# A decoder trunk on one core: another bank for the last half-columns, roots on ScalarE, residual sums as accumulating transfers, stores per row tile

## The chip, the core and the metric

The kernel runs on one core of one Trainium2 chip. The metric is the device time of one execution in microseconds; the median of several runs counts. TensorE (PE) multiplies, VectorE (DVE), ScalarE (ACT) and GpSimd (POOL) work on elements, and transfers are issued from the queues of SyncE (SP), ScalarE and GpSimd.

## The reference, cut to what matters

One layer, 512 tokens, 1024 channels, all in fp32. The parts that the change touches are the second norm, the down-projection with its residual sum, and the final norm:

```python
x = x + gate1 * (merged @ w_out[l])
h2 = _rmsnorm(x, norm2_g[l]) * (1.0 + scale2) + shift2
x = x + gate2 * _conv_ffn(h2, w_up[l], conv_w[l], conv_b[l], w_down[l])
...
return _rmsnorm(x, final_g)
```

`_rmsnorm` multiplies by `rsqrt(mean(x*x) + 1e-6)` and by a gain. `_conv_ffn` multiplies by w_up (1024 x 5632), puts a causal convolution of width 3 and a GELU on one half, multiplies by the other half, and multiplies by w_down (2816 x 1024).

## The kernel before

Every fp32 product is made of three: both operands are split into a rounded high part (cast on ScalarE) and the remainder (subtraction on VectorE; both in `split`, L101), and high by high, high by low and low by high are summed in PSUM.

The 512 tokens are four row tiles of 128. `x1` holds their residual stream in SBUF, [128, 4, 1024]. The up-projection and the down-projection are each done as seven block products instead of eight (a Strassen-like scheme), so sums and differences of blocks are needed as operands and of products afterwards. `mul_slot` (L1043) does the up-projection; the last 120 us are the down-projection.

The down-projection runs seven passes (L1473): m1, m5, m6, p2, p3, m7, p4. Each pass goes over the 2816 inner rows in six groups, five of two blocks and one of one (`grp`, L1420; NG = 6). For each group, `prepare` (L1626) splits the pass's operands: `ax` (pool tag gx, 5 buffers) and `wh`, `wl` (tags whi, wlo, WB = 3 buffers each). For some passes it also issues, on GpSimd, a transfer that adds another weight block onto the raw one (`accum_op=ALU.add`), for a later pass. Then `multiply` (L1642) does the products for u = 0 and 1, the two row tiles of one token half, into the pass's pair of PSUM banks: dX, dZ, dY, dW. A bank is 128 x 512.

`after_pass` (L1508) is a generator of small steps that turn finished banks into residual sums: subtract a bank, multiply by the gate, add to `x1`, take the square's row sum on ScalarE (`square`, L1485; its sum goes to `parts`), multiply by the final gain. The table `EACH` (L1658) says how many such steps are traced behind each group's `prepare` in the next pass. So steps from p2 run during p3, those from p3 during m7, those from m7 during p4. `e`, `e2` and `m1` are the buffers of differences.

The order of the instructions on VectorE, ScalarE, GpSimd and, here, TensorE is set by a planner that goes by the order of tracing and its own estimate of durations. Inside a `manual_schedule` block the order is that of the text. Two such blocks matter. The first (L1183 to L1380) holds the end of the output projection, the second norm and the start of the up-projection: `square2` (L1119), `norm_a` (L1125), `norm_b` (L1129). The second is `last_rows` (L1587): the last three groups (HOLD = 3) of the last pass, p4, and everything after them. There, TensorE finishes u = 0, then u = 1 in two column halves `c0` and `c1` of 256, both in bank dW[1]. `last_mul`, `last_add`, `last_gain`, `last_scale` and `last_scale2` (L1562 to L1585) turn the banks into output rows; `last_scale2` scales the second 512 columns on ScalarE and stores them from the queue that it is given.

The inverse root of a mean square is `rstd_start` (L136: the mean on VectorE, power -0.5 on GpSimd) and `rstd_end` (L146: a correction step in two VectorE instructions). The signs are arranged by factors -0.5 in the gains. The only activation tables needed before are those of Exp and Tanh, and from L1066 on that of Gelu.

Every engine, and every queue of transfers, takes its instructions in order: what waits holds up what stands behind it.

Of the kernel before, what the change touches and what calls it, by code (L numbers as in the profile page):

```python
# [8 lines left out]
F32 = mybir.dt.float32  # L9
# [5 lines left out]
P = 128  # L15
D = 1024
S = 512
# [26 lines left out]
def kernel(  # L44
# [101 lines left out]
    def rstd_end(dst, ms, r0, n, wpool):  # L146
        t = wpool.tile([P, n], F32, tag="rs_b", bufs=3, name="rt")
        if n == 1:
            nc.vector.scalar_tensor_tensor(t, r0, r0, ms, ALU.mult, ALU.mult)
        else:  # L150
            nc.vector.tensor_mul(t, r0, r0)
            nc.vector.tensor_mul(t, t, ms)
        nc.vector.scalar_tensor_tensor(dst, t, -3.0, r0, ALU.add, ALU.mult)

# [701 lines left out]
    while units or loaded or current or later:  # L856
        fill(1)
    for _ in ada:
        fill(1)
# [259 lines left out]
    def square2(t, hfs=(0, 1)):  # L1119
        for hf in hfs:  # L1120
            sq = big.tile([P, S], F32, tag="sq2", name=f"sqo{t}{hf}")
            ssq[t, hf] = bp.tile([P, 1], F32, tag="ss2", bufs=8, name=f"sso{t}{hf}")
            nc.scalar.activation(sq, x1[:, t, hf * S : (hf + 1) * S], AF.Square, accum_out=ssq[t, hf])  # L1123

    def norm_a(t):  # L1125
        nc.vector.tensor_scalar(ssq[t, 0], ssq[t, 0], 1.0 / D, EPS, ALU.mult, ALU.add)
        r2[t] = rstd_start(ssq[t, 1], 1, D, bp, plus=ssq[t, 0])

    def norm_b(t):  # L1129
        rs = bp.tile([P, 1], F32, tag="rs2", bufs=4, name=f"rso{t}")  # L1130
        rstd_end(rs, *r2[t], 1, bp)
        xns[t] = xnp[t // 2][:, t % 2]
        return rs
# [285 lines left out]

    grp = [(p, min(p + 2, NPR)) for p in range(0, NPR, 2)]  # L1420
# [70 lines left out]
    def stat_start(t):  # L1491
        a, b = parts[t, 0], parts[t, 1]
        nc.vector.tensor_scalar(a, a, 1.0 / D, EPS, ALU.mult, ALU.add)
        parts[t] = rstd_start(b, 1, D, bp, plus=a)

    def stat_end(t):
        rs = bp.tile([P, 1], F32, tag="rs2", bufs=4, name=f"rsd{t}")
        rstd_end(rs, *parts[t], 1, bp)
        return rs
# [8 lines left out]
    def after_pass(name):  # L1508
# [14 lines left out]
        elif name == "m7":  # L1523
# [4 lines left out]
            for u in two:  # L1528
                def add(u=u):
                    V.tensor_add(res(2 + u, 1), res(2 + u, 1), e2[:, u])  # L1530
                    square(2 + u, 1)
                yield add
            for u in two:
                def gain(u=u):
                    V.tensor_mul(e2[:, u], res(2 + u, 1), fgb[:, S:])
                    stat_start(u)
                yield gain
        elif name == "p3":
# [4 lines left out]
            for u in two:  # L1543
                def add(u=u):
                    V.tensor_add(res(u, 1), res(u, 1), e[:, u])
                    square(u, 1)
                yield add
            for u in two:
                yield lambda u=u: V.tensor_mul(res(u, 1), res(u, 1), fgb[:, S:])
        elif name == "p2":  # L1550
            for u in two:
                yield lambda u=u: V.tensor_mul(m1[:, u], dX[u], gate(0))
            for u in two:
                def add(u=u):
                    V.tensor_add(res(u, 0), res(u, 0), m1[:, u])
                    square(u, 0)
                yield add
# [4 lines left out]
    def last_mul(u, sl=slice(0, S)):  # L1562
        nc.vector.tensor_mul(m1[:, u, sl], dW[u][:, sl], gate(0)[:, sl])

    def last_add(u, sl=slice(0, S)):
        nc.vector.tensor_add(res(2 + u, 0)[:, sl], res(2 + u, 0)[:, sl], m1[:, u, sl])
        sq = big.tile([P, S], F32, tag="sq2", name=f"sqe{u}_{sl.start}")
# [19 lines left out]
    def last_rows(todo):  # L1587
# [8 lines left out]
        for sl in (c0, c1):  # L1596
            for g in todo:
                multiply(len(passes) - 1, g, 1, sl)
        for u in range(2):
            nc.scalar.activation(x1[:, u], x1[:, u], AF.Copy, scale=stat_end(u))  # L1600
# [41 lines left out]
    def multiply(i, g, u, sl=slice(0, S)):  # L1642
# [4 lines left out]
        for q in range(n):  # L1647
            first_mm = name in first and g == 0 and q == 0
            last_mm = g == len(grp) - 1 and q == n - 1
            for x, (a, b) in enumerate(((ah, wh), (ah, wl), (al, wh))):  # L1650
                nc.tensor.matmul(  # L1651
                    bank2[u][:, sl], a[:, q, cu], b[:, q, sl], start=first_mm and x == 0, stop=last_mm and x == 2,
                    skip_group_check=name not in first,
                )
# [65 lines left out]
```

## Time and profile before

| | us |
|---|---|
| runs shown: median (lowest to highest), 3 runs | 695.13 (693.9 to 696.05) |
| the profiled execution's own time | 695.11 |
| its span, first to last instruction | 693.3 |
| mean granted TensorE clock | 0.995 |
| TensorE busy | 676.6 (98%) |
| VectorE busy | 559.9 (81%) |
| ScalarE busy | 376.6 (54%) |
| GpSimd busy | 72.7 (10%) |

A row of the timeline gives the start in us from the span's beginning, the duration, the engine, the line of the program, the operation, output and inputs by name, the shapes, the number of instructions merged in the row, and in brackets the idle time just before with what ended it. A row of the chain gives start, length and whose time it is; "issue" is time in which nothing visible was waited for. A row of transfers gives target and source, the issuing queue, the count, the size of each and the median time from issue to landing. A "q" behind an engine's name is its sequencer.

### The profile page before, as it was taken

The page shows a single profiled execution, that of the slowest core. Times are in us where ns is not written, and L with a number is a line of the kernel's source. Part 1 is how long each engine was busy: PE and PEld are TensorE (multiplying, and loading weights), DVE is VectorE, ACT ScalarE, POOL GpSimd, SP SyncE. Part 2 cuts the span into 40 slices and gives each one's busy share as a digit, 9 for nine tenths or more (in the row PEclk, how much of TensorE's full clock was granted, in tenths as well). Part 3 has the DMA queues.
Part 4 walks back from the last instruction along what each step waited for, and adds up shares of the span by engine and source line. Part 5 has one row for each costly group of instructions (what it writes and reads, how often), then busy time and mean ns, then how long its engine had stood idle before and what let it go on. Part 6 is the DMA issues. An engine that isn't in the chain of part 4 may idle for free. (4 is left out here: it accounts for less than half of the span.)

```text
span 693.3 us, 10915 instructions
## 1 busy us (share of the span) xinstructions
PE 676.6 (98%) x4117; PEld 591.5 (85%) x4117; DVE 559.9 (81%) x1028; ACT 376.6 (54%) x661; POOL 72.7 (10%) x81
## 2 busy tenths in 40 slices
PE   8999999999999999999999999999999999999994
PEld 8787777778787888888799999999999998888873
DVE  4888887879787566663699898888888999979995
ACT  4656765354544333332487655665556565665663
POOL 2000000000100000000030101111111003431200
PEclk9999999999999999999999999999999999999997
DMA  9943544355254464258354988778867558996803
GB/s 351 407 166 108 185 134 151 122 172 158 97 178 156 142 222 152 93 186 245 115 108 133 217 212 197 188 194 185 204 172 185 140 177 204 196 205 182 144 1 122
DMA packets 71077, 119.68 MB, mean 173 GB/s; under 512 B 3952, under 2 KB 47728, under 8 KB 71024
## 3 DMA queue, kind: packets, MB, share of 16 engines
q1 hardware_dynamic: 52960, 95.04, 41.4%
q0 software_dynamic: 17776, 23.60, 20.6%
q8 instruction: 32, 0.52, 0.3%
q10 hardware_dynamic: 288, 0.34, 0.1%
q14 instruction: 21, 0.17, 0.1%
HBM read 116.87 MB, written 2.10 MB: 172 GB/s over the span
## 5 line engine op out<-in xcount | busy, mean ns | idle before, releaser
L1051 PE MATMUL up<-t,m_whi 128*128 128x256 f32 x528 | 96.1, 283 | 0.0
L1051 PEld LDWEIGHTS up<-t,m_whi 128*128 128x128 f32 x528 | 82.3, 192 | 0.0
L1051 PE MATMUL up<-t,m_wlo 128*128 128x256 f32 x264 | 74.6, 283 | 0.1
L1051 PE MATMUL up<-bh,p_wlo 128*128 128x256 f32 x232 | 65.7, 284 | 0.7 <-DVE p_wlo L994 0.7
L1051 PE MATMUL up<-bh,p_whi 128*128 128x256 f32 x232 | 65.6, 283 | 0.0
L1051 PE MATMUL up<-bl,p_whi 128*128 128x256 f32 x232 | 65.6, 283 | 0.0
L673 DVE CUSTOM_DVE_ANT_0 ra<-ra,csb 128x1024 f32<-128x1024 f32 x32 | 39.1, 1223 | 23.5 <-DMA ra<-in_w_ada_t_dram 23.2
L1051 PEld LDWEIGHTS up<-t,m_wlo 128*128 128x128 f32 x264 | 50.6, 192 | 0.3 <-DVE m_wlo L994 0.3
L1051 PEld LDWEIGHTS up<-bh,p_wlo 128*128 128x128 f32 x232 | 44.4, 192 | 1.1 <-DVE p_wlo L994 1.1
L1051 PEld LDWEIGHTS up<-bh,p_whi 128*128 128x128 f32 x232 | 44.5, 192 | 0.0
L1051 PEld LDWEIGHTS up<-bl,p_whi 128*128 128x128 f32 x232 | 44.5, 192 | 0.0
L962 POOL DMA_DIRECT2D s<-in_w_up_dram x21 | 27.1, 1363 | 156.0 <-DMA s<-in_w_up_dram 109.4
L143 POOL TENSOR_TENSOR r<-ms,mhalf 128x1 f32<-128x1 f32 (+1 forms) x13 | 11.8, 910 | 297.9 <-DVE ms L139 220.8
L994 DVE TENSOR_TENSOR m_wlo<-s,m_whi 128x1024 fp32r<-128x1024 f32 x31 | 37.8, 1220 | 2.0 <-ACT m_whi L990 2.0
L990 ACT CAST m_whi<-s 128x1024 fp32r<-128x1024 f32 x31 | 32.4, 1046 | 9.3 <-DVE s L984 6.0
L612 ACT ACTIVATE sd<-sd,dmx 128x128 f32<-128x128 f32 (+3 forms) x32 | 17.8, 556 | 29.8 <-DVE dmx L610 24.0
L1051 PE MATMUL up<-t,p_whi 128*128 128x256 f32 x176 | 32.2, 283 | 0.0
L1051 PEld LDWEIGHTS up<-t,p_whi 128*128 128x128 f32 x176 | 27.4, 192 | 0.2 <-issue 0.2
L1058 ACT ACTIVATE gT<-a,cols 128x512 f32<-128x512 f32 x22 | 17.7, 813 | 17.7 <-DVE a L1093 17.3
L990 ACT CAST p_whi<-wa 128x1024 fp32r<-128x1024 f32 x18 | 18.7, 1041 | 12.0 <-DMA s<-in_w_up_dram 8.9
L1051 PE MATMUL up<-t,p_wlo 128*128 128x256 f32 x88 | 24.9, 283 | 0.0
L994 DVE TENSOR_TENSOR p_wlo<-wa,p_whi 128x1024 fp32r<-128x1024 f32 x18 | 22.0, 1222 | 3.5 <-ACT p_whi L990 3.0
(497 smaller groups left out, 2010.0 us busy)
## 6 DMA issues: line engine op xcount, KB each, us to landing
ra<-in_w_ada_t_dram SPq DMA_DIRECT2D x32, 512.0 KB, 3.3
wa<-in_w_up_dram SPq DMA_DIRECT2D x22, 512.0 KB, 4.4
s<-in_w_up_dram SPq DMA_DIRECT2D x21, 512.0 KB, 4.7
s<-in_w_up_dram POOLq DMA_DIRECT2D x21, 512.0 KB, 6.1
adaw<-in_w_ada_t_dram SPq DMA_DIRECT2D x15, 512.0 KB, 9.8
a<-in_w_up_dram SPq DMA_DIRECT2D x11, 512.0 KB, 4.8
b<-in_w_down_dram SPq DMA_DIRECT2D x10, 512.0 KB, 4.3
w<-in_w_first_dram SPq DMA_DIRECT2D x8, 512.0 KB, 10.1
```

The source lines that it names most:

```text
L143: nc.gpsimd.tensor_tensor(r0, ms, mhalf[:, :n], ALU.pow)
L612: nc.scalar.activation(pm[m], pm[m], AF.Exp, bias=mx[:, m : m + 1], scale=slope, accum_out=lsum[:, m : m + 1])
L673: nc.vector.tensor_tensor_reduce(r, r, csb, 1.0, 0.0, ALU.mult, ALU.add, late_mod[:, idx : idx + 1])
L962: nc.gpsimd.dma_start(dst, upblock(*blk), accum_op=ALU.add)
L990: nc.scalar.copy(W[J, name][0], R[J, SRC[name]])
L994: nc.vector.tensor_sub(lo, R[J, SRC[name]], hi.bitcast(F32))
L1051: nc.tensor.matmul(o[u], w[:, k, cu], b[:, k], start=name in ("p1", "m5", "p2") and k == 0 and x == 0, stop=k == 3 and x == 2, skip_group_ ...
L1058: nc.scalar.activation(grow(j), av[J][:, u], AF.Identity, bias=cv[:, 66 + j : 67 + j], scale=cv[:, 44 + j : 45 + j])
```

## The change

- `root_start` and `root_end` are new: ScalarE's Sqrt of the mean square, then VectorE's reciprocal, then the same correction step. They take the place of GpSimd's power in the second norm (`norm_a`, `norm_b`), in the final norm of row tiles 0 and 1 (`stat_start`, `stat_end`) and in the tail. In the second norm the small `tensor_scalar` on the first half's sum moves from `norm_a` into `square2`, right behind its square.
- `root_table` is new: a Sqrt on one column, once behind the attention's last merge, once behind the last tile of the up-projection, which makes ScalarE load the root's table there.
- Six additions to `x1` on VectorE become transfers on GpSimd's queue that add onto `x1`; the squares follow them.
- In m7, groups 4 and 5 are multiplied first for u = 0 and then for u = 1; in p4 groups 0 and 1 likewise.
- In p4, groups 4 and 5 are followed by three steps instead of two: the two new ones (`row`) scale and store row tiles 0 and 1, which `last_rows` did.
- In `last_rows`, the last three groups of the columns `c1` of u = 1 are summed in bank dY[1]; dW[1] is multiplied and added over its whole width when `c0` is done, and `c1` is added afterwards. Row tile 2 is finished and stored between the two.

```diff
+    def root_start(ssq, d, wpool, plus):
+        r0 = wpool.tile([P, 1], F32, tag="rs_c", bufs=3, name="r0")
+        nc.scalar.activation(r0, ssq, AF.Sqrt, bias=plus, scale=1.0 / d)
+        ms = wpool.tile([P, 1], F32, tag="rs_a", bufs=3, name="ms")
+        nc.vector.scalar_tensor_tensor(ms, ssq, 1.0 / d, plus, ALU.mult, ALU.add)
+        return ms, r0
+
+    def root_end(dst, ms, r0, wpool):
+        nc.vector.reciprocal(r0, r0)
+        rstd_end(dst, ms, r0, 1, wpool)
+
+    def root_table(behind):
+        nc.scalar.activation(warm, behind, AF.Sqrt, scale=0.0)
...
+    root_table(tds[KT - 1][:, 0:1])
...
             nc.scalar.activation(sq, x1[:, t, hf * S : (hf + 1) * S], AF.Square, accum_out=ssq[t, hf])
+            if hf == 0:
+                nc.vector.tensor_scalar(ssq[t, 0], ssq[t, 0], 1.0 / D, EPS, ALU.mult, ALU.add)
 
     def norm_a(t):
-        nc.vector.tensor_scalar(ssq[t, 0], ssq[t, 0], 1.0 / D, EPS, ALU.mult, ALU.add)
-        r2[t] = rstd_start(ssq[t, 1], 1, D, bp, plus=ssq[t, 0])
+        r2[t] = root_start(ssq[t, 1], D, bp, ssq[t, 0])
...
+    root_table(grow(FT - 1)[:, 0:1])
...
                 def add(u=u):
-                    V.tensor_add(res(2 + u, 1), res(2 + u, 1), e2[:, u])
+                    nc.gpsimd.dma_start(res(2 + u, 1), e2[:, u], accum_op=ALU.add)
                     square(2 + u, 1)
                 yield add
             for u in two:
                 def gain(u=u):
+                    stat_start(u)
                     V.tensor_mul(e2[:, u], res(2 + u, 1), fgb[:, S:])
-                    stat_start(u)
                 yield gain
+            for u in two:
+                def row(u=u):
+                    nc.scalar.activation(x1[:, u], x1[:, u], AF.Copy, scale=stat_end(u))
+                    nc.sync.dma_start(od[u * P : (u + 1) * P, :], x1[:, u])
+                yield row
...
-                    V.tensor_add(res(u, 1), res(u, 1), e[:, u])
+                    nc.gpsimd.dma_start(res(u, 1), e[:, u], accum_op=ALU.add)
...
-                    V.tensor_add(res(u, 0), res(u, 0), m1[:, u])
+                    nc.gpsimd.dma_start(res(u, 0), m1[:, u], accum_op=ALU.add)
...
         for g in todo:
             multiply(len(passes) - 1, g, 0)
-        for sl in (c0, c1):
-            for g in todo:
-                multiply(len(passes) - 1, g, 1, sl)
-        for u in range(2):
-            nc.scalar.activation(x1[:, u], x1[:, u], AF.Copy, scale=stat_end(u))
-            nc.sync.dma_start(od[u * P : (u + 1) * P, :], x1[:, u])
-        last_mul(0)
-        s0 = last_add(0)
-        last_gain(0)
-        last_mul(1, c0)
-        r0 = rstd_start(s0, 1, D, bp, plus=part[0])
-        s1 = last_add(1, c0)
-        last_gain(1, c0)
+        for g in todo:
+            multiply(len(passes) - 1, g, 1, c0)
+        for g in todo:
+            multiply(len(passes) - 1, g, 1, c1, dY[1], g == todo[0])
+        last_mul(0, dW[0])
+        last_add(0)
+        s0 = last_square(0)
+        last_mul(1, dW[1])
+        r0 = root_start(s0, D, bp, part[0])
         rs0 = bp.tile([P, 1], F32, tag="rs2", bufs=4, name="rse0")
-        rstd_end(rs0, *r0, 1, bp)
+        root_end(rs0, *r0, bp)
+        last_add(1)
+        last_scale2(0, rs0, nc.sync)
+        s1 = last_square(1, c0)
+        nc.vector.scalar_tensor_tensor(res(2, 0), res(2, 0), rs0, fgb[:, :S], ALU.mult, ALU.mult)
+        nc.sync.dma_start(od[2 * P : 3 * P, :S], res(2, 0))
+        last_mul(1, dY[1], c1)
+        last_add(1, c1)
+        s2 = last_square(1, c1)
         partial(s1, part[1])
-        last_mul(1, c1)
-        s2 = last_add(1, c1)
-        r1 = rstd_start(s2, 1, D, bp, plus=s1)
-        last_gain(1, c1)
-        last_scale(0, rs0)
-        last_scale2(0, rs0, nc.sync)
+        last_gain(1)
+        r1 = root_start(s2, D, bp, s1)
         rs1 = bp.tile([P, 1], F32, tag="rs2", bufs=4, name="rse1")
-        rstd_end(rs1, *r1, 1, bp)
+        root_end(rs1, *r1, bp)
         last_scale(1, rs1)
         last_scale2(1, rs1, nc.scalar)
...
-    EACH = {3: (0, 2, 2, 2, 1, 1), 4: (0, 0, 1, 1, 2, 2), 5: (0, 0, 2, 2, 2, 2), 6: (0, 0, 2, 2, 2, 2)}
+    EACH = {3: (0, 2, 2, 2, 1, 1), 4: (0, 0, 1, 1, 2, 2), 5: (0, 0, 2, 2, 2, 2), 6: (0, 0, 2, 2, 3, 3)}
...
+        together = {"m7": (4, 5), "p4": (0, 1)}.get(passes[i][0], ())
         for g in range(NG - tail):
             for u in range(2):
-                multiply(i, g, u)
+                for gg in together if g in together[:1] else () if g in together else (g,):
+                    multiply(i, gg, u)
```

`last_add` loses its square, which becomes `last_square`; `last_mul` takes the bank, and `multiply` takes an optional bank and a flag that starts it afresh.

More of the change, by code (lines that the diff above doesn't have):

```diff
@@ L1493, in stat_start @@
         nc.vector.tensor_scalar(a, a, 1.0 / D, EPS, ALU.mult, ALU.add)
-        parts[t] = rstd_start(b, 1, D, bp, plus=a)
+        parts[t] = root_start(b, D, bp, a)
     def stat_end(t):
         rs = bp.tile([P, 1], F32, tag="rs2", bufs=4, name=f"rsd{t}")
-        rstd_end(rs, *parts[t], 1, bp)
+        root_end(rs, *parts[t], bp)
         return rs
@@ L1559, in after_pass, with last_mul, last_square @@
                 yield lambda u=u: V.tensor_mul(res(u, 0), res(u, 0), fgb[:, :S])
-    def last_mul(u, sl=slice(0, S)):
-        nc.vector.tensor_mul(m1[:, u, sl], dW[u][:, sl], gate(0)[:, sl])
+    def last_mul(u, src, sl=slice(0, S)):
+        nc.vector.tensor_mul(m1[:, u, sl], src[:, sl], gate(0)[:, sl])
     def last_add(u, sl=slice(0, S)):
         nc.vector.tensor_add(res(2 + u, 0)[:, sl], res(2 + u, 0)[:, sl], m1[:, u, sl])
+    def last_square(u, sl=slice(0, S)):
         sq = big.tile([P, S], F32, tag="sq2", name=f"sqe{u}_{sl.start}")
@@ L1640, in prepare, with multiply @@
         ops[i, g] = ah, al, wh, wl
-    def multiply(i, g, u, sl=slice(0, S)):
+    def multiply(i, g, u, sl=slice(0, S), o=None, fresh=False):
         name, bank2 = passes[i][:2]
@@ L1647, in multiply @@
         for q in range(n):
-            first_mm = name in first and g == 0 and q == 0
+            first_mm = (name in first and g == 0 or fresh) and q == 0
             last_mm = g == len(grp) - 1 and q == n - 1
@@ L1651, in multiply @@
                 nc.tensor.matmul(
-                    bank2[u][:, sl], a[:, q, cu], b[:, q, sl], start=first_mm and x == 0, stop=last_mm and x == 2,
-                    skip_group_check=name not in first,
+                    (bank2[u] if o is None else o)[:, sl], a[:, q, cu], b[:, q, sl], start=first_mm and x == 0, stop=last_mm and x == 2,
+                    skip_group_check=name not in first and o is None,
                 )
```

2 lines of the change are left out of this document (1 added, 1 removed).

## The prediction, made before the changed kernel ran

> **What bounds the kernel now.** I read the chain of waits first, from its end backwards, because it says which engine each stretch is worth anything on.
>
> ```profile
> 393.81 184.34 PE up L1051 x1534
> 578.15 89.12 PE dc L1651 x393
> 667.27 0.02 issue
> 667.29 0.70 DVE chain_outl L1525
> 667.99 0.14 issue
> 668.13 15.45 PE dc L1651 x81
> ...
> 687.16 0.66 POOLq L1716
> ...
> 688.29 0.72 ACT x L1584
> ```
>
> From 393.81 to 667.27 TensorE is the chain without a break. Whatever VectorE, ScalarE or GpSimd save there is worth nothing, and whatever they lose counts only once TensorE stands still. There is one small hole, where pass p4 waits for VectorE's subtraction from its bank (667.29). At 668.13 + 15.45 = 683.58 TensorE is done, and a serial tail of 5.4 us follows to 688.29 + 0.72 = 689.01, then the last store. So the change can gain in the tail, at the hole, and before 393.81, and it can lose anywhere. Next, the tail in the timeline:
>
> ```profile
> 680.01 0.69 DVE L1563 TENSOR_TENSOR pairs<-dc,g2row 128x512 f32<-128x512 f32 x1
> 679.69 2.20 ACT L1600 ACTIVATE x<-x,rsd 128x1024 f32<-128x1024 f32 x2 [1.79 <-DVE rsd L153]
> 681.79 0.62 ACT L1569 ACTIVATE sqe<-x 128x512 f32<-128x512 f32 x1
> 683.60 0.42 DVE L1563 TENSOR_TENSOR pairs<-dc,g2row 128x256 f32<-128x256 f32 x1 [1.44 <-PE dc L1651]
> 685.37 0.41 DVE L1563 TENSOR_TENSOR pairs<-dc,g2row 128x256 f32<-128x256 f32 x1
> 686.34 0.42 ACT L1569 ACTIVATE sqe<-x 128x256 f32<-128x256 f32 x1 [1.25 <-DVE x L1566]
> 686.66 0.19 ACT L1569 ACTIVATION_READ_ACCUMULATOR sqe<-x 128x1 f32 x1
> 687.84 0.22 DVE L149 SCALAR_TENSOR_TENSOR rt<-r,ms 128x1 f32<-128x1 f32 x1
> 688.10 0.16 DVE L153 SCALAR_TENSOR_TENSOR rse<-rt,r 128x1 f32<-128x1 f32 x1
> ```
>
> The reader is to see three things. The first half of the last columns is finished about midway between 680.0 and 683.58, near 681.8, but VectorE takes it up only at 683.60, when TensorE leaves the bank. So both halves (683.60 and 685.37) stand behind the end. Row tile 2's square waits until 681.79 although its input is ready near 681.45, since ScalarE is scaling row tiles 0 and 1. And from the last square (686.85) to the scale (688.29) pass 1.44 us, 0.66 of them in GpSimd's power.
>
> **The tail, part by part.** Prices that it needs:
>
> ```profile
> L504 ACT ACTIVATE es<-nm,sink x8: 282/290/298, 68.7 to 111.5; 128x4 f32<-128x4 f32 x8
> L213 DVE RECIPROCAL cs<-cs x1: 202/202/202, 5.9 to 5.9; 128x8 f32<-128x8 f32 x1
> 680.74 0.69 DVE L1566 TENSOR_TENSOR x<-x,pairs 128x512 f32<-128x512 f32 x1
> ```
>
> No square root stands in the trace. The nearest row is a small ScalarE activation with a bias column, 0.29 us; I take that. A root is then 0.03 hand-over + 0.29 + 0.04 + reciprocal 0.20 + 0.22 + 0.16, with 0.03 between: 1.03 us in place of 1.44.
>
> Walk of the new order, TensorE ending as now. Row tile 2: product and sum until 681.43 as before; its square starts at 681.48, if the scalings of row tiles 0 and 1 are gone by then, and is read at 682.2. Meanwhile VectorE multiplies the whole of dW[1] (0.69, from 681.8 to 682.5); the half that has no final sum yet is just the earlier groups' part. Root of tile 2: Sqrt until 682.5, reciprocal and the two corrections until 683.2. Full-width sum of tile 3 until 683.9, fused scale and store of tile 2's first half until 684.5 (0.69 each, small overlap). Then the last half from its own bank: product 0.42 and sum 0.42 with their hand-overs until 685.3, square and read-out 0.51 until 685.8, root until 686.8, ScalarE's scale 0.72 until 687.5. Before, that ended at 689.01: **-1.5 us**. Bounds: -0.7, if the scalings still hold ScalarE until 681.9 and the small steps don't overlap; -2.0, if VectorE finds the c1 work first.
>
> The last store goes by two rows:
>
> ```profile
> out_dram<-x SPq DMA_DIRECT2D x3, 256.0 KB, 2.1
> out_dram<-x ACTq DMA_DIRECT2D x1, 256.0 KB, 3.3
> ```
>
> Now four stores of 256 KB leave within 1.6 us (687.5 to 689.04) and the last pays 3.3. Afterwards tile 2's halves leave near 684 and only two go at the end. I take 2.5, nearer to the first row, since only one neighbour is left: **-0.8**, bounds -1.2 and 0. The 0.9 us behind the landing stay.
>
> **The hole at p4.** p4's 15.45 us hold 51 full and 30 half products, 0.23 for a full one. With groups 4 and 5 together, bank 0 of m7 is complete nine products (2.1 us) before the pass ends, where it was three. It was complete at 667.27; three products of bank 1 follow, so p4 could start near 667.8 and starts at 668.13: the hole is 0.35, and the subtraction now fits ahead of it. But the weight buffers are three: p4's group 1 takes the one that m7's group 4 frees, now three products (0.7) later, and it is wanted six products (1.4 us) earlier (group 1 follows group 0 on the same bank). Cast 1.05 and low part 1.22 from 667.3 give 669.6 to 669.8, against a need at 669.4. That returns 0.2 to 0.4. I take **-0.2**, bounds -0.35 and +0.5.
>
> **Roots in the middle.** They stand at the second norm, where VectorE and ScalarE, not TensorE, set the pace:
>
> ```profile
> 347.07 0.99 PE L1146 MATMUL th<-ident,xn 128*128 128x128 f32 x7 [0.65 <-DVE xn L1136]
> 352.72 0.63 ACT L1123 ACTIVATE sqo<-x 128x512 f32<-128x512 f32 x1 [0.53 <-DVE x L1117]
> 393.81 0.39 PE L1051 MATMUL up<-bh,p_wlo 128*128 128x256 f32 x1 [0.34 <-DVE p_wlo L994]
> ```
>
> Two quicker roots bring row tile 1's norm forward by about 0.6 and close the first hole. But the moved tensor_scalar now stands in VectorE's queue ahead of add_x(3, 1) and waits for the square before it (about +0.3), and the Sqrt of tile 3 stands in ScalarE's queue ahead of the early casts (+0.3). Both eat the lead before the hole at 393.81, which is what the rest hangs on. I take **0**, bounds -0.6 and +0.4.
>
> **Tables.** Two loads of the root's table are new.
>
> ```profile
> 385.63 1.28 ACT L1066 ACT_TABLE_LOAD   x1
> 386.92 0.63 ACT L1066 ACTIVATE gT<-gT 128x512 f32<-128x512 f32 x1
> 311.66 1.05 ACT L102 CAST wo_h<-wo 128x1024 fp32r<-128x1024 f32 x1 [3.37 <-PE oc L1111]
> 583.65 1.06 ACT L102 CAST m1wh<-chain_outh 128x1024 fp32r<-128x1024 f32 x1 [1.36 <-PE dc L1651]
> 585.77 1.22 DVE L103 TENSOR_TENSOR m1wl<-chain_outh,m1wh 128x1024 fp32r<-128x1024 f32 x1
> ```
>
> A load and a Sqrt are 1.28 + 0.29 = 1.57. The first root_table follows tile 7's merge into a ScalarE idle of 3.37; the second follows the last up-projection tile into an idle of 1.36, so a weight cast slips by 0.2 to 584.9, and VectorE takes that cast up only at 585.77. **0**, bounds 0 and +0.5; without that cover it would be 1.6 each. The Trainium skill, page "ScalarE: Activation LUTs", section "What ACT_TABLE_LOAD costs", adds a drain of about 1.38 us to every switch; by it the second load would reach 1.6 us past its gap, for which I would add up to 0.5. The trace's load in mid-program lasts 1.28 us and its activation follows 0.01 later (386.92), so the rows speak against the drain.
>
> **The six sums as transfers.** Each takes a 0.69 us addition off VectorE, where it is hidden anyway, and puts an issue on GpSimd and a landing in front of a ScalarE square and a VectorE product. The rows:
>
> ```profile
> b<-in_w_down_dram POOLq DMA_DIRECT2D x5, 512.0 KB, 6.8
> b<-in_w_down_dram POOLq DMA_DIRECT2D x1, 256.0 KB, 7.3
> 640.85 0.69 DVE L1552 TENSOR_TENSOR pairs<-dc,g2row 128x512 f32<-128x512 f32 x1
> 641.24 1.20 POOL L1637 DMA_DIRECT2D b<-in_w_down_dram  x1 [0.52 <-DVE p3wl L103]
> 645.59 0.63 ACT L1488 ACTIVATE sqd<-x 128x512 f32<-128x512 f32 x1
> 646.22 0.62 ACT L102 CAST p3wh<-b 128x512 fp32r<-128x512 f32 x1
> 648.93 1.05 ACT L102 CAST m7wh<-b 128x1024 fp32r<-128x1024 f32 x1 [1.58 <-PE dc L1651]
> 652.82 0.39 PE L1651 MATMUL dc<-m7wh,m7a 128*128 128x512 f32 x1
> ```
>
> Pass p3 is the tight one, because its six weight accumulates use the same queue. The second product of p2 is ready at 641.54; issued behind the transfer of 641.24 it starts at 642.5, and with 7 to 8 us lands near 650. Its square stood at 645.59. ScalarE takes its queue in order: behind the square stand p3's last cast (646.22; TensorE wants it six products before 652.82, at 651.5) and m7's first (648.93, with its low part wanted at 653.0). A landing by 650 lets both pass with a few tenths. In m7 and p4 the queue is otherwise empty; landings of 4 to 6 us from the products fall near 664 and 678, ahead of 667.8 and of the tail's start at 680. I take **0**; from below no gain is possible while TensorE is the chain, from above the price is the slower rival.
>
> **Sum.** -1.5 - 0.8 - 0.2 = -2.5 on a profiled execution of 695.11 us (span 693.3 and 1.8 around it): **692.6**. The median of the runs shown is 695.13, so no correction.
>
> **Rivals.** *Slower: ScalarE stands at a square whose transfer is late.* Place: pass p3, the square of row tile 1. If the planner sets the transfers behind group 4's accumulate (issue near 647.5) or the queue is as full as 7.3 us for 256 KB suggests, they land at 654 to 657, and if the square keeps its place at 645.6, cast, low part (0.69) and TensorE follow it. Every microsecond past about 650.5 is one lost: from 655.1 on it costs 4.6 and the kernel is slower by over 0.3% (692.6 + 4.6 = 697.2); 657 costs 6.5, 699.1. For it: POOL's landings of 6.8 and 7.3 in this stretch. Against it: the planner may place square and products later, and nothing needs them before the tail. *A part of that*: landings near 652, or p4's square ahead of its last weight cast, lose 1 to 2.5: 693.9 to 695.4. *A thinner tail*: c1's work waits behind row tile 2's root on VectorE, and the store keeps its 3.3: -0.7 to -1.2, 693.9 to 694.4; for it, VectorE's four dependent small steps; against it, the walk above already has them. *The change doesn't do what it says*: if the tracker holds the read of dW[1] until dY[1]'s products end too, the half-columns stay serial and only the quicker root (0.4) and part of the store remain: 694.2; two separate banks speak against it.
>
> **How the numbers follow.** Chances: the forecast 0.50, the partly late transfers 0.20, the slower one 0.18, the thinner tail or the unhelpful bank 0.12. A measurement here tells about 0.3%, 2.1 us, from no change, so faster means below 693.0 and slower above 697.2. The forecast's own range is 691.3 to 693.6 (its bounds don't all fall to one side); some eight tenths of it lie below 693.0, which gives faster 0.40; its rest, the partly late transfers and the thinner tail make same 0.42; the slower rival 0.18. The range goes from 691.3 up to 697.0: it takes in the two rivals in between and leaves out most of the slower one.
>
> **What would show it.** After: the second square-and-scale chain behind TensorE's end 1.3 to 1.7 us shorter; the product from dW[1] starting about 681.8 in old time, before TensorE ends; the last store landing in under 3 us; p4's hole gone or moved to its group 1; two more table loads in idle time; TensorE still unbroken from 394 to 667. It is wrong if TensorE's wait list in p3, m7 or p4 names a cast or low part, with ScalarE's squares waiting for a transfer just ahead.

## The result and the profile after

Over nine runs each, the changed kernel took 698.77 us (696.6 to 700.39) and the kernel before 694.6 us (692.98 to 696.46). The ratio is 1.0058, 95% interval 1.0041 to 1.0076: slower by some 4 us. The profiled execution took 698.77 us; its span is 697.0, against 693.3.

TensorE's first product of each stage cuts both spans into the same pieces, so one subtraction says where the time went:

| stretch, us | before | after | difference |
|---|---|---|---|
| up to the output projection's first product | 305.65 | 305.27 | -0.38 |
| output projection, to the first transpose | 40.50 | 42.56 | +2.06 |
| second norm, to the first up product | 5.96 | 6.12 | +0.16 |
| up-projection | 225.88 | 226.47 | +0.59 |
| m1, m5, m6, p2 | 59.87 | 59.88 | +0.01 |
| p3 | 14.96 | 16.40 | +1.44 |
| m7 | 15.31 | 16.63 | +1.32 |
| p4 | 15.43 | 15.54 | +0.11 |
| tail, to ScalarE's last scaling | 5.45 | 4.04 | -1.41 |
| last store to the end | 4.32 | 4.09 | -0.23 |

The chain of waits of the changed kernel:

```profile
396.24 184.34 PE up L1066 x1534
580.58 44.26 PE dc L1675 x195
...
644.41 1.41 POOL x L1577
...
662.86 3.32 DMA x<-chain_kvB
...
670.77 1.22 DVE p4wl L103
673.33 11.96 PE dc L1675 x51
```

Before, TensorE carried the chain alone from 393.81 to 667.27. Now it leaves TensorE near 625 and comes back at 673.33, and GpSimd's issue of a residual sum (`x`, 644.41) and the landing of another (662.86) stand in between. TensorE's waits in the timeline of the changed kernel:

```profile
336.27 0.51 PE L1122 MATMUL oc<-wo_h,mg3h 128*128 128x512 f32 x1 [0.54 <-ACT wo_h L102]
337.72 0.50 PE L1123 MATMUL oc<-wo_l,mg3h 128*128 128x512 f32 x1 [0.95 <-DVE wo_l L103]
...
654.61 0.49 PE L1675 MATMUL dc<-p3wh,p3a 128*128 128x512 f32 x1 [0.55 <-ACT p3wh L102]
655.43 0.50 PE L1675 MATMUL dc<-p3wl,p3a 128*128 128x512 f32 x1 [0.33 <-DVE p3wl L103]
657.35 0.50 PE L1675 MATMUL dc<-m7wl,m7a 128*128 128x512 f32 x1 [0.26 <-DVE m7wl L103]
673.33 0.47 PE L1675 MATMUL dc<-p4wh,p4a 128*128 128x512 f32 x1 [0.96 <-DVE chain_outl L1542]
```

Each names a cast or a low part, or the subtraction ahead of p4. Two groups are to be explained: the output projection's, which the sum did not have, and p3's with what follows. For p3, the timeline of ScalarE, VectorE and GpSimd in the changed kernel:

```profile
643.69 1.21 POOL L1661 DMA_DIRECT2D b<-in_w_down_dram  x1 [0.51 <-DVE p3wl L103]
644.41 1.41 POOL L1577 DMA_DIRECT2D x<-pairs  x1
...
646.68 0.63 ACT L1505 ACTIVATE sqd<-x 128x512 f32<-128x512 f32 x1 [2.40 <-DMA x<-pairs]
653.33 0.63 ACT L1505 ACTIVATE sqd<-x 128x512 f32<-128x512 f32 x1 [4.16 <-DMA x<-pairs]
653.96 0.60 ACT L102 CAST p3wh<-b 128x512 fp32r<-128x512 f32 x1
654.09 0.69 DVE L1581 TENSOR_TENSOR x<-x,fgbr 128x512 f32<-128x512 f32 x1 [3.53 <-ACT sqd L1505]
654.70 0.68 DVE L103 TENSOR_TENSOR p3wl<-b,p3wh 128x512 fp32r<-128x512 f32 x1
```

p3 starts at 640.30 here and at 637.86 before, so a time in p3 is set back by 2.44 us to compare it with the kernel before. The second sum is issued at 644.41, behind a weight accumulate, and ScalarE's square of row tile 1 waits for it until 653.33. Right behind the square stands p3's last cast, which TensorE wants; on VectorE the product by the final gain waits for the square, and the low part stands behind that. For the output projection, the same view, first of the changed kernel:

```profile
322.17 2.64 POOL L977 DMA_DIRECT2D s<-in_w_up_dram  x2 [11.73 <-PE oc L1126]
...
327.71 1.05 ACT L102 CAST wo_h<-wo 128x1024 fp32r<-128x1024 f32 x1
334.22 1.05 ACT L102 CAST early<-wa 128x1024 fp32r<-128x1024 f32 x1 [5.46 <-DMA wa<-in_w_up_dram]
335.18 1.04 ACT L102 CAST wo_h<-wo 128x1024 fp32r<-128x1024 f32 x1
```

and of the kernel before:

```profile
329.41 1.05 ACT L102 CAST early<-wa 128x1024 fp32r<-128x1024 f32 x1 [0.37 <-DMA wa<-in_w_up_dram]
333.42 1.05 ACT L102 CAST wo_h<-wo 128x1024 fp32r<-128x1024 f32 x1 [2.96 <-PE oc L1111]
...
353.78 0.54 POOL L143 TENSOR_TENSOR r<-ms,mhalf 128x1 f32<-128x1 f32 x1 [2.55 <-DVE ms L141]
354.29 4.06 POOL L962 DMA_DIRECT2D s<-in_w_up_dram  x3
```

Before, GpSimd's next accumulating loads of up weights (`s`) stood behind the second norm's four powers and left at 354.29. With the powers gone they leave at 322.17. The weight load that ScalarE's early cast waits for then lands by 334.22 in place of 329.41, and the output projection's last cast, behind it in order, moves from 333.42 to 335.18. (The output projection starts 0.38 us earlier in the changed kernel, so the landing is 5.2 us later, measured from there.) The tail, on the other hand, does what was forecast; the changed kernel's timeline:

```profile
687.11 0.69 DVE L1585 TENSOR_TENSOR pairs<-dc,g2row 128x512 f32<-128x512 f32 x1 [0.38 <-PE dc L1675]
...
691.00 0.19 ACT L1593 ACTIVATION_READ_ACCUMULATOR sqe<-x 128x1 f32 x1
691.22 0.29 ACT L157 ACTIVATE r<-sse,sse 128x1 f32<-128x1 f32 x1
691.54 0.16 DVE L163 RECIPROCAL r<-r 128x1 f32<-128x1 f32 x1 [0.17 <-ACT r L157]
692.00 0.16 DVE L153 SCALAR_TENSOR_TENSOR rse<-rt,r 128x1 f32<-128x1 f32 x1
692.19 0.72 ACT L1608 ACTIVATE x<-chain_outl,rse 128x512 f32<-128x512 f32 x1 [0.68 <-DVE rse L153]
```

The read-out of dW[1] at 687.11 comes 1.8 us before TensorE's end at 688.87, and the root takes 1.00 us from 691.19 to 692.19.

### The profile page after: what moved, and what is told of

Read it like the earlier page. It is cut to its first block, busy times and chain, and to the rows that moved or that the text cites. A ratio compares the mean times of both kernels' runs of the same rounds, so it can differ in the third digit from the quotient of the medians.

```text
span 697.0 us, 10933 instructions
## 1 busy us (share of the span) xinstructions
PE 676.9 (97%) x4117; PEld 589.7 (85%) x4117; DVE 557.0 (80%) x1028; ACT 380.8 (55%) x673; POOL 73.4 (11%) x79
## 4 chain that ended last, share of the span: by engine, by line
PE 66%; DVE 14%; DMA 8%; issue 5%; ACT 5%; POOL 1%; SPq 0%; ACTq 0%; DVEq 0%; POOLq 0%
PE up L1066 26%; PE dc L1675 8%; PE av L322 3%; DMA ra<-in_w_ada_t_dram 2%; PE pgd L106 2%; PE pgd L107 2%; PE pgd L108 2%; DMA wa<-in_w_up_dram 2%; PE pga L106 1%; PE aqa L319 1%; DMA adaw<-in_w_ada_t_dram 1%; PE pga L108 1%; PE pga L107 1%; DVE ra L687 1%; PE pB L107 1%
## 5 line engine op out<-in xcount | busy, mean ns | idle before, releaser
L626 ACT ACTIVATE sd<-sd,dmx 128x128 f32<-128x128 f32 (+3 forms) x32 | 17.8, 556 | 30.0 <-DVE dmx L624 24.2
L143 POOL TENSOR_TENSOR r<-ms,mhalf 128x4 f32<-128x4 f32 x5 | 6.5, 1294 | 219.6 <-DVE ms L139 219.6
```

The costliest lines, as they stand in the source:

```text
L626: nc.scalar.activation(pm[m], pm[m], AF.Exp, bias=mx[:, m : m + 1], scale=slope, accum_out=lsum[:, m : m + 1])
```

## The experiments

Each is the changed kernel with the edit shown, and "the run with the hold" is the base of the later ones. Ratios are to the kernel before, run beside it on the same chip; the runs from the tied squares on were made on another chip than those ahead of them, so their times are compared by these ratios and their stages by the traces. Stage lengths are those of one profiled execution. Theory A: the freed GpSimd queue cost the first 2 to 3 us. Theory C: the squares that wait for a landing cost the rest. Rivals: ScalarE's roots, or chance in the loads, cost by themselves (B), the order of p4's steps costs (D), the transfers cost by the queue and the DMA engines.

**Sums back on VectorE**, all six:

```diff
-                    nc.gpsimd.dma_start(res(u, 0), m1[:, u], accum_op=ALU.add)
+                    V.tensor_add(res(u, 0), res(u, 0), m1[:, u])
```

> The changed kernel with its six residual sums put back on VectorE (tensor_add in place of the accumulating transfers); the rest of the change stays. Theory C, the squares of ScalarE wait for the landing of the sums, and casts stand behind them: the three gaps of TensorE near 655-657 go, p4's first product comes near 670.5 (668.13 before, 673.33 in the changed kernel), what is left is the 1.5 to 2.4 us lost by 396, and the time is 3 us under the changed kernel's, 695.3 to 696.3 us, 1.001 to 1.003 of before. Rival D, the order of p4's steps costs it (the two row scalings of 2.19 us on ScalarE between p4's casts, groups 0 and 1 taken together): the hole ahead of p4's first product stays near 1 us, and the time is 697.3 us or more.

695.62 us, ratio 1.002 (1.0009 to 1.0031). p3 takes 14.96, m7 14.97, p4 15.38, and TensorE waits for nothing in them. Theory C holds as far as the sums go, and D falls: the order of p4's steps is the changed one. The early loss stayed and was larger in this profile: output projection 41.60, norm 7.88.

**Powers back in the second norm**:

```diff
-        r2[t] = root_start(ssq[t, 1], D, bp, ssq[t, 0])
+        r2[t] = rstd_start(ssq[t, 1], 1, D, bp, plus=ssq[t, 0])
```

> The changed kernel with the middle norm's four roots put back to GpSimd's power (and its table load left out); transfers, tail and order of p4 stay. Theory A, the powers had held the up weights' accumulating transfers back on GpSimd's queue, and without them these collide with the plain weight load that ScalarE's early cast waits for: the load issued near 324.5 lands near 329.4 again (334.19 in the changed kernel), TensorE's gaps of 0.54 and 0.95 us near 337 go, the up chain's last stretch starts near 393.8 (396.24), and the time is 1.5 to 2.4 us under the changed kernel's, 696.4 to 697.3 us. Rival B, the time was lost by ScalarE's roots themselves or by chance in the loads: the gaps near 337 stay in place and the time is within 0.5 us of 698.8.

696.3 us, ratio 1.002 (1.0008 to 1.0031), just under the expected range. The output projection takes 40.52 again and its two gaps are gone, as theory A has it. The up chain's last stretch starts at 395.22, not 393.8: the norm took 7.31 us in this profile.

**Both edits together**:

> Both put back: sums on VectorE, middle norm by GpSimd's power; what stays of the change is the tail (second half of the last columns in its own bank, roots by ScalarE), the row tiles stored behind their roots in p4, and groups taken together. Theories A and C together: 693.0 us, 1.6 under before (the tail's 1.4 and the closing's 0.2), 0.9975 of before, with no new gap of TensorE. If rival D holds, p4's hole stays and the time is 694 to 694.8 us, no faster than before.

692.53 us, ratio 0.9969 (0.9957 to 0.9981): faster than before, by what the tail brings and a little more. p3 and m7 take 14.96 each, tail and store 4.17 and 4.14. The two losses add up to the whole.

**Roots on ScalarE, and a power that nothing reads beside each**:

```diff
         r2[t] = root_start(ssq[t, 1], D, bp, ssq[t, 0])
+        idle = bp.tile([P, 1], F32, tag='rs_d', bufs=2, name='idle')
+        nc.gpsimd.tensor_tensor(idle, r2[t][0], mhalf[:, :1], ALU.pow)
```

> The changed kernel with the middle roots kept on ScalarE, and beside each of the four a power issued on GpSimd as before, on a tile that nothing reads, so that GpSimd's queue has the order of before. Theory A: the up weights' accumulates wait behind the powers again, the load lands near 329.4, the gaps near 337 go, the up chain's last stretch starts at 393.2 to 394.0, and the time is 696.2 to 696.9 us, equal to the run with the powers in use or a few tenths less. Rival B: gaps near 337 stay, up chain from 396, 698.3 to 699 us.

696.14 us, ratio 1.0016 (1.0007 to 1.0025). The output projection takes 40.52, the norm 5.12, and the up chain's last stretch starts at 391.84. With the same roots as the changed kernel and only GpSimd's order restored, the early loss is gone: B falls. Over all profiles the output projection takes 40.50 to 40.52 where GpSimd's loads are held back, and 42.56 and 41.60 in the two where they are not, so chance in the loads does not explain it. p3 and m7 lose as before (17.03 and 16.65).

**One power behind the last root, sums on VectorE** (the run with the hold):

```diff
+        if t == NT - 1:
+            hold = bp.tile([P, 1], F32, tag="rs_d", bufs=1, name="hold")
+            nc.gpsimd.tensor_tensor(hold, r2[t][0], mhalf[:, :1], ALU.pow)
```

> The changed kernel with the six sums on VectorE, the middle roots on ScalarE, and one power issued on GpSimd behind the last middle root (on a tile that nothing reads), which holds the up weights' accumulates back as before. If one instruction that waits is all that the order needs, the output projection takes 40.5 us from its first product to the first transpose (40.50 before, 42.56 changed), the up stage to the down projection 225.9, p3 and m7 14.96 each, and the time is 691.5 to 692.5 us, equal to the run with both put back or up to 1 us under it, as the shorter root chain may close part of TensorE's 0.65 us gap ahead of the transposes. Rival: ScalarE's roots in the middle cost by themselves, and the time is 694 or more.

691.94 us, ratio 0.9958 (0.9944 to 0.9972), the lowest of all. Its timeline shows the hold at work:

```profile
328.15 1.05 ACT L102 CAST early<-wa 128x1024 fp32r<-128x1024 f32 x1
332.56 1.05 ACT L102 CAST wo_h<-wo 128x1024 fp32r<-128x1024 f32 x1 [3.35 <-PE oc L1126]
...
351.86 0.57 POOL L1146 TENSOR_TENSOR hold<-ms,mhalf 128x1 f32<-128x1 f32 x1 [42.06 <-DVE ms L159]
352.39 4.06 POOL L977 DMA_DIRECT2D s<-in_w_up_dram  x3
```

GpSimd waits 42.06 us for a number nobody wants, the loads leave at 352.39, the early cast waits for nothing, and the output projection's cast waits only for TensorE. The interval overlaps that of the run with both put back, so ScalarE's roots in the second norm are not shown to be worth anything by the time; the traces below show what they save.

**Which sums?** Only p2's two as transfers, then only p3's and m7's four, both on the run with the hold:

> As the run with the hold, with only p2's two sums as accumulating transfers (these run in p3); p3's and m7's stay on VectorE. Theory C, the second landing is late for ScalarE's square in p3: p3 takes 16.4 us in place of 14.96, m7 stays at 14.96 to 15.3, and the time is 1.4 to 1.8 us over the run with the hold. Rival, the losses came from all six together on GpSimd's queue and the DMA engines: p3 takes under 15.5.

695.71 us, ratio 1.0016 (1.0003 to 1.0029). p3 takes 16.37 as expected, but m7 takes 16.37 too, and the time is 3.8 us over the run with the hold, not 1.4 to 1.8.

> As the run with the hold, with p3's and m7's four sums as accumulating transfers and p2's two on VectorE. Theory C: p3 takes 14.96, m7 16.6 (p3's squares stand ahead of the casts for p4, so VectorE's subtraction that p4's first product waits for comes late, gap near 1 us), p4 15.5, which is m7's sums' whole cost, 0.1 to 0.2; the time is 1.6 to 1.9 us over the run with the hold. Rival, the hole at p4 was only what p3's delay left behind: m7 takes 15.3 or less.

692.15 us, ratio 0.9967 (0.9952 to 0.9982). Busy times by stretch, the rows being p3, m7 and p4 (length, then TensorE, its weight loads, VectorE, ScalarE and GpSimd with their counts, clock, DMA share, GB/s). Only p2's sums as transfers:

```profile
636.35:652.72 16.37, 15.52 (x67) 12.31 (x66) 10.84 (x17) 8.82 (x16) 7.99 (x8) 1.00 1.01 180
652.72:669.09 16.37, 15.42 (x67) 12.15 (x66) 16.37 (x26) 11.49 (x20) 0.00 (x0) 1.00 0.17 30
```

Only p3's and m7's:

```profile
638.33:653.29 14.96, 14.96 (x67) 12.39 (x66) 13.53 (x21) 9.83 (x17) 6.15 (x6) 1.00 1.00 175
653.29:668.29 15.00, 15.00 (x67) 12.23 (x66) 14.43 (x28) 11.70 (x20) 1.73 (x2) 1.00 0.33 65
668.29:684.07 15.78, 15.78 (x82) 12.97 (x81) 13.09 (x23) 8.06 (x16) 1.72 (x2) 1.00 0.34 90
```

And the run with the hold, for comparison:

```profile
636.27:651.23 14.96, 14.96 (x67) 12.39 (x66) 13.53 (x21) 9.84 (x17) 6.15 (x6) 1.00 1.01 172
651.23:666.19 14.96, 14.96 (x67) 12.39 (x66) 14.96 (x24) 9.95 (x18) 0.00 (x0) 1.00 0.12 21
```

The second expectation was wrong where it gave p3's sums a hole of their own: m7 takes 15.00, and the time is 0.2 us over the run with the hold, as the rival has it. p2's two sums alone cost both stages, 1.41 in p3 and 1.41 in m7. The rows show how one late landing is paid twice. Held up behind the square, VectorE does 10.84 us of work in p3 in place of 13.53, about 1.3 us of that difference being the two additions; the rest is left for m7, where VectorE was full already (14.96 of 14.96) and is full again, at 16.37 of 16.37.

**The squares one pass later**, with the counts in `EACH` shifted to match:

```diff
-                    square(u, 0)
                 yield add
...
         elif name == "p3":
...
+            for u in two:
+                yield lambda u=u: square(u, 0)
```

> As the run with only p2's sums as transfers, but their two squares and two gains stand one pass later in ScalarE's and VectorE's order, behind the first casts of m7, when both transfers have landed. Theory C, it is the place of the waiting square in ScalarE's order that costs, not the transfer: p3 takes 14.96 to 15.1 again and the time is within 0.5 us of the run with the hold. Rival, the transfers cost by what they take from the queue and the DMA engines (the accumulates of m7's weights land later behind them): p3 or m7 still takes over 15.7, and the time is a us or more over the run with the hold.

695.86 us, ratio 1.001 (0.9995 to 1.0025); p3 16.48, m7 16.35. It looks like a win for the rival, but the timeline shows that nothing had moved:

```profile
650.34 0.63 ACT L1508 ACTIVATE sqd<-x 128x512 f32<-128x512 f32 x1 [4.62 <-DMA x<-pairs]
...
650.97 0.60 ACT L102 CAST p3wh<-b 128x512 fp32r<-128x512 f32 x1
651.09 0.69 DVE L1569 TENSOR_TENSOR x<-x,fgbr 128x512 f32<-128x512 f32 x1 [4.04 <-ACT sqd L1508]
```

The square was traced a pass later, and the planner set it ahead of p3's last cast again. The run tells nothing between the theories.

**The squares tied behind a cast of m7**, all six sums as transfers, with the hold (`issue_after` makes the planner keep the order; `EACH` is shifted much as in the run before, where it changed nothing):

```diff
+                    with tc.issue_after(casts["m7", 2].ins):
+                        square(u, 0)
+                    with tc.issue_after(lows["m7", 2].ins):
+                        V.tensor_mul(res(u, 0), res(u, 0), fgb[:, :S])
```

> The run with the hold, with all six sums as accumulating transfers, as the change has them, but p2's two squares and two gains are tied behind the cast and the low part of m7's group 2 on ScalarE and VectorE (in the run before them the scheduler had put the squares back where they were, ahead of the last cast of p3). Theory C, the instructions that wait in order cost, not the transfers: p3 takes 14.96 to 15.1, m7 15.0 to 15.4, p4 15.5 to 15.8, and the time is 691.8 to 693 us. Rival, the transfers cost by the queue and the DMA engines: p3 takes 16 or more, and the time is 694 or more.

693.87 us, ratio 0.9982 (0.9972 to 0.9993). Its p3 and m7:

```profile
637.84:652.80 14.96, 14.96 (x67) 12.39 (x66) 11.18 (x15) 8.70 (x13) 7.99 (x8) 1.00 1.02 177
652.80:668.59 15.79, 15.12 (x67) 12.23 (x66) 15.22 (x26) 11.67 (x23) 1.72 (x2) 1.00 0.46 82
```

GpSimd issues the same eight transfers in p3 (7.99 us), with the DMA engines as busy (1.02), and p3 takes 14.96. So in p3 the order costs, not the transfers. m7 took 0.4 more than expected and 0.83 more than with the hold alone, which stays partly open: TensorE waits 0.67 us there ahead of p4, for a step of VectorE that follows p3's squares, and these still wait 1.42 us for their transfers. The time is 0.9 us over the expected range, between the two theories' ranges; the norm's stretch, 6.26 in this profile, was 1.15 longer than with the hold alone. By the ratios all six sums as transfers stay behind all six on VectorE (0.9982 against 0.9958, with intervals that just touch).

**The norm ahead of the early cast**, with the hold:

```diff
-    hi_early(1)
-    lo_early(1, slice(0, 4))
     for k in last:
         out_step(0, k)
...
     norm_c(0, norm_b(0))
+    hi_early(1)
+    lo_early(1, slice(0, 4))
     hi_early(2)
```

> The run with the hold, with the cast and the low part of the first up weight (the load that lands last there) moved behind row tile 0's norm on ScalarE and VectorE. If the landing of that load is what makes the stretch from the first transpose to the first up product vary from 5.1 to 7.9 us between runs, it is 5.0 to 5.2 here whatever the landing, and the time is 0 to 1 us under the run with the hold, 691 to 692 us. Rival: the cast comes late for the up chain now, and the gap moves there; the time is 692 to 693 us.

692.98 us, ratio 0.9967 (0.9955 to 0.9979), in the rival's range. The norm's stretch took 5.56, neither the 5.0 to 5.2 expected nor a gain, and the up-projection 226.48. The run can't answer its question: the load landed early in this profile, 28.8 us after the output projection's first product, when it holds nothing up. The traces of the other runs answer it. The columns are the root's engine, the start of the early cast that waits for this load, counted from the output projection's first product, and the time from there to the first up product:

| run | roots of the second norm | early cast, us | to the first up product, us |
|---|---|---|---|
| before | GpSimd | 30.25 | 16.21 |
| both put back | GpSimd | 31.26 | 16.20 |
| powers back | GpSimd | 31.58 | 16.25 |
| one bank (below) | ScalarE | 30.42 | 15.48 |
| p3's and m7's sums as transfers | ScalarE | 30.92 | 15.51 |
| squares tied | ScalarE | 31.26 | 15.52 |
| changed kernel | ScalarE | 33.17 | 15.51 |
| sums back | ScalarE | 34.00 | 15.48 |

The two runs with equal starts, both put back and squares tied, show the cast as follows:

```profile
336.83 1.05 ACT L1202 CAST early<-wa 128x1024 fp32r<-128x1024 f32 x1 [2.41 <-DMA wa<-in_w_up_dram]
335.95 1.05 ACT L1207 CAST early<-wa 128x1024 fp32r<-128x1024 f32 x1 [2.41 <-DMA wa<-in_w_up_dram]
```

So in these runs the distance is fixed for each kind of root, the landing sets when the up-projection starts, and ScalarE's roots shorten the distance by 0.7 us. In the six runs with ScalarE's roots and GpSimd's queue held in which the cast starts at 28.7 to 29.7, the first up product comes 45.6 us after the output projection's first: there something else limits, and the norm's stretch is 5.11 to 5.12. Why the load lands earlier or later from run to run stays open, and so does the up-projection's half microsecond: where it takes 226.5 in place of 225.9 it has one more wait of 0.4 us near its start.

**Three terms of the sum.** Groups no longer taken together, and the down projection's roots by GpSimd's power (with the hold; there are four, not the six that the expectation names); then the grouping alone; then the last columns in one bank, with the read-outs to match:

```diff
-        together = {"m7": (4, 5), "p4": (0, 1)}.get(passes[i][0], ())
+        together = ()
...
-        parts[t] = root_start(b, D, bp, a)
+        parts[t] = rstd_start(b, 1, D, bp, plus=a)
...
-            multiply(len(passes) - 1, g, 1, c1, dY[1], g == todo[0])
+            multiply(len(passes) - 1, g, 1, c1)
```

> The run with the hold, with groups no longer taken together around m7 and p4, and the six roots of the down projection's norm put back to GpSimd's power: two terms of the prediction, read from two stages. The hole ahead of p4's first product was put at 0.2: m7 takes 15.2 to 15.3 in place of 14.96. ScalarE's root was put at 0.41 under GpSimd's: the stretch from TensorE's end to ScalarE's last scaling is 4.5 in place of 4.1. The time is 0.5 to 0.8 us over the run with the hold. If either stretch is unchanged, that term of the sum was worth nothing.

694.38 us, ratio 0.9995 (0.9984 to 1.0006); m7 16.31, tail 4.81: all three are beyond what was expected.

> The run with the hold, with groups no longer taken together around m7 and p4, and ScalarE's roots everywhere. In the run that also had GpSimd's roots, two of VectorE's instructions stood waiting for these roots ahead of the subtraction that p4's first product waits for, so its hole of 1.18 us belongs to both edits. If taking the groups together is what closes the hole, m7 takes 15.3 to 15.9 here in place of 14.96 and the time is 0.3 to 0.9 us over the run with the hold, 692.2 to 692.9 us. Rival: GpSimd's roots alone made the hole, and m7 takes under 15.1.

692.37 us, ratio 0.9974 (0.9962 to 0.9985); m7 15.39. Against 14.96, taking the groups together is worth 0.43 us. The other 0.92 of the 16.31 is GpSimd's: two corrections on VectorE wait for its powers ahead of the subtraction.

> The run with the hold, with the second half of the last columns summed in the same bank as the first again. The own bank was put at about 1.1 us of the tail's 1.5: the stretch from TensorE's end to ScalarE's last scaling is 5.1 to 5.2 in place of 4.1, as row tile 3's first read-out waits for the end of TensorE, and the time is 1 us over the run with the hold. Rival: the read-out of one half never waited for the products of the other, and the stretch stays under 4.4.

693.2 us, ratio 0.9973 (0.9963 to 0.9984); tail 5.17 against 4.12 with the hold. The own bank is worth 1.05 us, as the prediction's walk had it.

## Why the prediction was wrong

**The tail** was right: -1.5 predicted, -1.41 measured, with a root of 1.00 us where 1.03 was worked out. Taken away one at a time, own bank and roots cost 1.05 and 0.69; the root's share had been put at 0.41. The trace shows one reason why it counts more than once: VectorE's sum of row tile 3 stands behind row tile 2's root: with GpSimd's power that sum starts 0.02 us before TensorE's end, with the hold 0.35 before it.

**The last store** was mis-sized: -0.8 predicted, -0.23 measured. The transfers view of the changed kernel:

```profile
out_dram<-x SPq DMA_DIRECT2D x3, 256.0 KB, 2.0
out_dram<-x ACTq DMA_DIRECT2D x1, 256.0 KB, 3.1
```

The store from ScalarE's queue lands after 3.1 us even with a single neighbour. I had put its 3.3 down to the company of three. What makes it slower than the others no run isolates.

**The hole at p4** was given -0.2. With the sums in time it is -0.35 (15.31 to 14.96 in the run with the hold); in the changed kernel VectorE's backlog pushed the subtraction back (672.50, TensorE at 673.33) and hid it.

**The tables** cost nothing, as predicted. The second load in the changed kernel:

```profile
584.44 1.28 ACT L167 ACT_TABLE_LOAD   x1
585.73 0.20 ACT L167 ACTIVATE warm<-gT 128x1 f32<-128x1 f32 x1
```

It takes 1.28 us, the activation follows 0.01 later, and m1 to p2 keep 59.88 us. The drain of 1.38 us that the Trainium skill, page "ScalarE: Activation LUTs", section "What ACT_TABLE_LOAD costs", would add does not appear.

**The roots in the middle** were given 0, bounds -0.6 and +0.4. The step that failed is the list of costs: I costed what the roots add to VectorE and ScalarE, but not what the removed powers had been holding. GpSimd's queue was read in p3 only, where the change adds to it, and not at the norm, where the change takes from it. The early stages lost 2.81 us in the table (2.06, 0.16 and 0.59), and one restored instruction on GpSimd's queue removes the 2.06 whole (40.50 in the run with the hold). The first two together are 2.22: the early cast of the table above starts 2.92 later (33.17 against 30.25), and the quicker roots win back 0.70. The forecast's "by about 0.6" for the roots was right, then, but it was buried under the landing. The 0.59 is not settled.

**The six sums** were given 0, on "issued behind the transfer of 641.24 it starts at 642.5, and with 7 to 8 us lands near 650" and on "A landing by 650 lets both pass with a few tenths". The place in the queue was right: 644.41 in the changed kernel is 641.97 on the clock of the kernel before, right behind that transfer. The landing took 8.9 us to its reader in place of 7 to 8: ScalarE had it at 653.33, which is 650.89, some 0.9 later than forecast. By the prediction's own price, one microsecond lost for each past about 650.5, that costs 0.4; p3 lost 1.44. The step that failed is this slack. It counts the square and the cast that TensorE wants, but puts p3's last low part at nothing. From ScalarE's start on the square to TensorE's product with that low part pass 2.10 us (653.33 to 655.43), and in the kernel before that product starts at

```profile
651.68 0.39 PE L1651 MATMUL dc<-p3wl,p3a 128*128 128x512 f32 x1
```

so the landing was wanted by 649.6, not 650.5. The run with the idle powers bears this out: its square starts 0.64 later in p3 than in the changed kernel (13.67 after p3's start against 13.03), and p3 is 0.63 longer. The second step that failed is a path that the prediction does not have: VectorE, which falls behind in p3, pays again in m7, 1.32 against the kernel before and 1.67 against the run with the hold.

Of the rivals, the slower one named the place and the engine that waits, but its landings of 654 to 657 did not come. In size it was the partly late one, with 1 to 2.5 for the sums against 1.44 + 1.32 = 2.76. That the total of 698.77 fell where the slower rival had put it (697.2 to 699.1) is chance: it took the early loss as well, which no rival had. The transfers view of the changed kernel:

```profile
x<-pairs POOLq DMA_DIRECT2D x2, 256.0 KB, 7.3
x<-chain_kvB POOLq DMA_DIRECT2D x2, 256.0 KB, 3.3
x<-chain_outl POOLq DMA_DIRECT2D x2, 256.0 KB, 3.3
```

In m7 and p4 "the queue is otherwise empty" held: the four sums cost 0.04 in m7 and 0.37 in p4 in the run that had them alone.

With the sums put back and GpSimd's order kept, the kernel takes 691.94 us, 2.4 under the 694.36 of the kernel before beside it, where the forecast had 2.5 under. That the two agree is partly luck: by the profiles of the run with the hold, tail, store and hole bring 1.33, 0.18 and 0.35, which is 1.9 in place of 2.5, and the norm's stretch, given 0, brings 0.85.

## What to carry to other kernels

An instruction that is removed from an in-order queue sets free whatever stood behind it: read what comes next on that engine, when it will start, and what it will meet. A sum handed to a transfer is only free if it lands before its reader's turn, or if nothing that is wanted soon stands behind the reader; price the landing with every transfer ahead of it in the queue, and tie the reader behind the work that can't wait. When two profiles are compared, set both to the start of the stage before reading how late something is. After an experiment that moves an instruction, look in the trace whether it moved.

## What the runs showed of the hardware

An accumulating transfer of 256 KB from one SBUF buffer onto another lands 3.3 us after its issue with no weight accumulates in its queue, and 7.3 us (the median of two, 5.9 and 8.8) after it among 512 KB weight accumulates. The Trainium skill, page "DMA: Bandwidth & Descriptors", section "Anatomy of one DMA — SWDGE (gpsimd) path", gives 2.0 us and the bytes by 436e3 per us, an estimate of 2.6 us; the trace is 0.7 over it with the queue empty and nearly three times as long in p3. Two accumulating loads of 512 KB that left at 322.17 made a plain load of 512 KB on another queue land 4 to 5 us later: by the cast that waits for it, 28.9 us after the output projection's first product in the changed kernel and 28.0 with the sums back, against 23.3 to 24.2 in the other runs, which all hold these loads back.
